# Staggered tile addresses: 160 bytes of padding behind activation and split-weight tiles in a two-layer decoder trunk

## The chip, the cores and the metric

The kernel runs on one core of a Trainium2 chip. The metric is the device time of one execution in microseconds (us); lower is better. Engines are named as the profile names them: PE is TensorE's matmuls, PEld its loads of the stationary operand, DVE is VectorE, ACT is ScalarE, POOL is GpSimd, and SP is the queue that issues most transfers.

## What is computed

The reference is a trunk of two decoder layers on 256 tokens of width 2048, in float32:

```python
for l in range(DEPTH):                      # DEPTH = 2
    h = _rmsnorm(x, norm1_g[l])
    if l % 2 == 0:
        x = x + _conv_diff_mixer(h, ...)    # projections to 6144 columns, conv, differential attention
    else:
        x = x + _fox_mixer(h, ...)          # 16 heads of 128, forgetting attention
    h = _rmsnorm(x, norm2_g[l])
    x = x + _sqrelu_mlp(h, mlp_w1[l], mlp_w2[l])   # hidden 8192
```

Nearly all work is matrix products of a 256-row activation with weights that are read once: a projection to 6144 columns, an output projection of 2048x2048, and an MLP of 2048x8192 and 8192x2048 in each layer.

## The kernel before

Every weight and every activation is used as a sum of two float32r numbers, a high part and a low part (float32r: the trace has one record for such a matmul, and two for one of plain float32). A product then takes three matmul terms: high by high, high by low and low by high. The tiles of interest are these:

- `act`: made in `ActT` (lines 103 to 111), 128 partitions by 4 k-tiles by {high, low} by 256 tokens, 8192 bytes in each partition. The pool `actp` has 9 buffers.
- `raw`: 8192 bytes of weights as they come from memory, 3 buffers, filled by SP's queue (lines 134, 136 and 517).
- `wh` and `wl`: the high and the low part of half a `raw`, 4096 bytes each, 4 buffers each. ACT makes `wh` by a copy that rounds (lines 142 and 524), DVE makes `wl` by a subtraction (lines 143 and 525).

Two routines do the products. `gemm` (lines 124 to 154) computes tokens by 512 output columns: the stationary operand is 128 columns of `act`, the moving operand is 512 columns of `wh` or `wl`, so lines 149, 150 and 151 are matmuls of 128x512. `gemm_t` (lines 510 to 536), used for the first product of each MLP, computes the transposed output: the stationary operand is 128 columns of `wh` (line 530) or `wl` (line 534), the moving operand is 512 columns of `act` (high and low side by side) or 256 columns of its high part. Each matmul is preceded by its own load of a 128x128 stationary operand, which runs while the matmul before it is still streaming.

Work that is not a product (norms, attention, convolution) is written as generators in the list `pending`; `step()` advances one of them after each half `raw`, and `until()` advances them until an activation is ready. This order is fixed when the program is built. A small product for the forget gates (`forget_gates`, lines 405 and 406) has slices of one constant tile `gws` as its stationary operand, which start 128 bytes apart.

Pools hand out addresses one behind the other. All larger tiles are multiples of 512 bytes long, so in the built program each `ident`, `xr`, `act`, `raw`, `wh`, `wl`, `q`, `k`, `v`, `junk`, `s` and `pT` starts at an address that is 128 modulo 512; `ones` and `triu` start at 32 modulo 512. The last tile ends at byte 227,648 of a partition, and the first 16,384 bytes are a scratch area for DMA descriptors that GpSimd would write.

Of the kernel before, what the change touches and what calls it, by code (L numbers as in the profile page):

```python
# [8 lines left out]
F32 = mybir.dt.float32  # L9
F32R = mybir.dt.float32r  # L10
# [6 lines left out]
P = 128  # L17
D = 2048
KT = D // P
CW = 512  # L20
# [6 lines left out]
def trunk_kernel(  # L27
# [7 lines left out]
    nc = tc.nc  # L35

    const = ctx.enter_context(tc.tile_pool(name="const", bufs=1))
    resid = ctx.enter_context(tc.tile_pool(name="resid", bufs=1))
    actp = ctx.enter_context(tc.tile_pool(name="actp", bufs=9))
    wraw = ctx.enter_context(tc.tile_pool(name="wraw", bufs=3))  # L40
    wspl = ctx.enter_context(tc.tile_pool(name="wspl", bufs=4))
# [8 lines left out]
    xr = [resid.tile([P, 2, CW], F32, name=f"xr{n}") for n in range(NCH)]  # L50
    xv = x[0].rearrange("(t p) d -> p t d", p=P)
    ident = const.tile([P, P], F32, name="ident")
    nc.scalar.dma_start(ident, eye)
    grow = work.tile([P, 2 * P], F32, name="y")[:32, :P]
    nc.sync.dma_start(grow, norm1_g.rearrange("l (k p) -> (l k) p", p=P))
# [21 lines left out]
    def step():  # L77

        while pending:
            try:  # L80
                next(pending[0])
                return True
            except StopIteration:
                pending.pop(0)
        return False

    def until(done):
        while not done():
            assert step()
# [13 lines left out]
    class ActT:  # L103


        def __init__(self, row):
            self.row = row
            self.left = 4
            self.both = actp.tile([P, 4, 2, 2 * P], F32R, name="act")
            self.hi = self.both[:, :, 0, :]  # L110
            self.lo = self.both[:, :, 1, :]

# [11 lines left out]
    def gemm(acts, w, c0, first=False):  # L124

        acc = [accp.tile([P, CW], F32, name="acc") for _ in range(2)]
        total = 4 * len(acts)
        i = 0
        for ai, a in enumerate(acts):
            raw = wraw.tile([P, 4, CW], F32, name="raw")  # L130
            src = w[a.row:a.row + CW, c0:c0 + CW].rearrange("(k p) n -> p k n", p=P)
            if first and ai == 0:
                for h in range(2):
                    nc.sync.dma_start(raw[:, 2 * h:2 * h + 2, :], src[:, 2 * h:2 * h + 2, :])
            else:
                nc.sync.dma_start(raw, src)
            until(lambda: a.left <= 0)
            for h in range(2):
                wh = wspl.tile([P, 2, CW], F32R, name="wh")
                wl = wspl.tile([P, 2, CW], F32R, name="wl")  # L140
                rw = raw[:, 2 * h:2 * h + 2, :]
                nc.scalar.copy(wh, rw)  # L142
                nc.vector.tensor_tensor(wl, rw, wh.bitcast(F32), ALU.subtract)  # L143
                for t in range(2):
                    ts = slice(t * P, (t + 1) * P)
                    for j in range(2):
                        k = 2 * h + j
                        st, sp = i + j == 0, i + j == total - 1
                        nc.tensor.matmul(acc[t], a.hi[:, k, ts], wh[:, j, :], start=st, stop=False)  # L149
                        nc.tensor.matmul(acc[t], a.hi[:, k, ts], wl[:, j, :], start=False, stop=False)  # L150
                        nc.tensor.matmul(acc[t], a.lo[:, k, ts], wh[:, j, :], start=False, stop=sp)  # L151
                i += 2
                step()
        return acc
# [36 lines left out]
    def proj(nm, w, c0, name, first=False):  # L191

        acc = gemm(nm.acts, w, c0, first)
        o = qkv.tile([P, 2, CW], F32, name=name)
        for t in range(2):
            nc.scalar.activation(o[:, t, :], acc[t], AF.Copy, scale=nm.r(t))
        return o
# [302 lines left out]
    def out_proj(acts, w, nxt):  # L500

        for part in (acts[:-1], acts[-1:]):
            for n in range(NCH):
                acc = gemm(part, w, n * CW)
                for t in range(2):
                    nc.vector.tensor_tensor(xr[n][:, t, :], acc[t], xr[n][:, t, :], ALU.add)
                if len(part) == 1:
                    pending.append(nxt.chunk(n))

    def gemm_t(acts, w, c0):  # L510


        acc = [accp.tile([P, CW], F32, name="acc") for _ in range(2)]
        for c in range(2):
            raw = wraw.tile([P, 8, 2 * P], F32, name="raw")
            r0 = c * 8 * P
            nc.sync.dma_start(raw, w[r0:r0 + 8 * P, c0:c0 + 2 * P].rearrange("(k p) n -> p k n", p=P))
            for h in range(2):
                a = acts[2 * c + h]
                until(lambda: a.left <= 0)  # L520
                wh = wspl.tile([P, 4, 2 * P], F32R, name="wh")
                wl = wspl.tile([P, 4, 2 * P], F32R, name="wl")
                rw = raw[:, 4 * h:4 * h + 4, :]
                nc.scalar.copy(wh, rw)  # L524
                nc.vector.tensor_tensor(wl, rw, wh.bitcast(F32), ALU.subtract)  # L525
                for f in range(2):
                    fs = slice(f * P, (f + 1) * P)
                    for k in range(4):
                        st = c + h + k == 0
                        nc.tensor.matmul(  # L530
                            acc[f], wh[:, k, fs], a.both[:, k, :, :].rearrange("p s t -> p (s t)"), start=st, stop=False)
                    for k in range(4):
                        sp = (c, h, k) == (1, 1, 3)
                        nc.tensor.matmul(acc[f][:, 2 * P:], wl[:, k, fs], a.hi[:, k, :], start=False, stop=sp)  # L534
                step()
        return acc

    def mlp(nm, l, nxt):
        ov = out[0].rearrange("(t p) d -> p t d", p=P)
        for g in range(4):  # L540
            hT = []
            for n in range(4):
                c0 = (4 * g + n) * CW
                a = ActT(c0)
                for i in range(2):
                    acc = gemm_t(nm.acts, mlp_w1[l], c0 + 2 * i * P)

                    r = work.tile([P, 2, 2 * P], F32, name="junk")
                    for f in range(2):
                        nc.scalar.copy(r[:, f, :], acc[f][:, 2 * P:])  # L550
                        nc.vector.tensor_tensor(r[:, f, :], acc[f][:, :2 * P], r[:, f, :], ALU.add)  # L551
                    nc.vector.scalar_tensor_tensor(r, r, 0.0, r, ALU.max, ALU.mult)  # L552
                    a.split((slice(None), slice(2 * i, 2 * i + 2)), r, None, 2)
                hT.append(a)
            if g == 0:
                r2 = small.tile([P, 2], F32, name="r2", bufs=3)
                for t in range(2):
                    nc.vector.tensor_tensor(r2[:, t:t + 1], nm.r(t), nm.r(t), ALU.mult)
            for n in range(NCH):
                acc = gemm(hT, mlp_w2[l], n * CW)  # L560
                for t in range(2):
                    nc.vector.scalar_tensor_tensor(  # L562
                        xr[n][:, t, :], acc[t], r2[:, t:t + 1], xr[n][:, t, :], ALU.mult, ALU.add)
                    if g == 3 and nxt is None:
                        q = nc.sync if t == 0 else nc.scalar
                        q.dma_start(ov[:, t, n * CW:(n + 1) * CW], xr[n][:, t, :])
                if g == 3 and nxt is not None:
                    pending.append(nxt.chunk(n))
# [11 lines left out]
    for g in range(2):  # L580
        q = proj(nm, w, 3 * C + g * CW, "q", first=g == 0)
        k = proj(nm, w, 4 * C + g * CW, "k")
# [16 lines left out]
    for g in range(4):  # L599
# [3 lines left out]
        k = proj(nm, w, D + g * CW, "k")  # L603
# [37 lines left out]
```

## Time and profile before

| | |
|---|---|
| Median of 3 runs | 2211.32 us (2210.77 to 2211.58) |
| Profiled execution: time / span of its instructions | 2211.69 us / 2210.0 us |
| PE busy, PEld busy | 100%, 84% of the span |
| DVE busy, ACT busy, POOL busy | 59%, 47%, 1% |
| Memory traffic | 412 MB, 186 GB/s |

The table is read as a statement about who could be late: an engine that is busy for the whole span leaves nothing for the others to delay, and then the question is how long its own instructions take. A matmul's duration in the profile includes its way through the array, so durations of successive matmuls overlap; what a matmul costs is the distance from its start to the next start, which the timeline view shows to 0.01 us.

### The profile page before, as it was taken

To read this page: it belongs to the slowest core of one execution; us is meant where nothing else is said; L and a number is where in the kernel's file an instruction comes from. 1 tells how busy PE (TensorE), PEld (TensorE's weight loads), DVE (VectorE), ACT (ScalarE), POOL (GpSimd) and SP (SyncE) were. 2 spreads that over 40 slices of the span, in tenths; PEclk is the share of its full clock that TensorE was granted. 3 is DMA by queue.
4 is the path that set the end of the run, shared out by engine and by line. 5 is a ranking of instruction groups with operands and counts; after the bars stand their busy time and mean duration, and the time that the engine had idled before them with its cause. 6 is when DMAs were issued, how large, how long until landed. Compare 5 with 4: busy or idle time off the path is not lost.

```text
span 2210.0 us, 26959 instructions
## 1 busy us (share of the span) xinstructions
PE 2199.4 (100%) x10868; PEld 1850.6 (84%) x10868; DVE 1293.1 (59%) x1608; ACT 1037.9 (47%) x1415; POOL 12.6 (1%) x17
## 2 busy tenths in 40 slices
PE   8999999999999999999999999999999999999999
PEld 7887888888888888888888888888888888888887
DVE  5676665655565565565556565666555655655654
ACT  6555544543443444344445455445434444444443
POOL 0000000000000000000000000000000000000000
PEclk9999999999999999999999999999999999999999
DMA  7554555665665665665555555555656656656664
GB/s 254 172 166 160 188 182 189 182 191 191 191 191 190 190 191 190 191 191 190 180 175 194 186 183 171 189 170 175 189 191 192 189 191 193 189 191 194 187 200 143
DMA packets 278015, 412.14 MB, mean 186 GB/s; under 512 B 9367, under 2 KB 144770, under 8 KB 277890
## 3 DMA queue, kind: packets, MB, share of 16 engines
q1 hardware_dynamic: 270032, 405.84, 58.2%
q10 hardware_dynamic: 7858, 4.58, 0.7%
q8 instruction: 85, 1.39, 0.3%
q14 instruction: 40, 0.33, 0.0%
HBM read 408.28 MB, written 2.11 MB: 186 GB/s over the span
## 4 chain that ended last, share of the span: by engine, by line
PE 99%; ACT 0%; DMA 0%; DVE 0%; SPq 0%; issue 0%
PE acc L530 22%; PE acc L149 21%; PE acc L151 21%; PE acc L150 21%; PE acc L534 11%; PE tp L170 1%; PE tp L286 0%; PE tp L298 0%; PE tp L474 0%; PE tp L494 0%; DMA xr<-in_x_dram 0%; PE tp L495 0%; PE tp L473 0%; PE tp L372 0%; PE tp L322 0%; PE tp L321 0%
## 5 line engine op out<-in xcount | busy, mean ns | idle before, releaser
L143 DVE TENSOR_TENSOR wl<-raw,wh 128x1024 fp32r<-128x1024 f32 x512 | 629.5, 1231 | 559.9 <-ACT wh L142 559.4
L142 ACT CAST wh<-raw 128x1024 fp32r<-128x1024 f32 x512 | 538.2, 1052 | 719.8 <-PE acc L151 637.0
L149 PE MATMUL acc<-wh,act 128*128 128x512 f32 x2048 | 812.9, 397 | 2.0 <-ACT wh L142 2.0
L151 PE MATMUL acc<-wh,act 128*128 128x512 f32 x2048 | 799.9, 391 | 0.0
L150 PE MATMUL acc<-wl,act 128*128 128x512 f32 x2048 | 798.7, 390 | 0.0
L530 PE MATMUL acc<-act,wh 128*128 128x512 f32 x2048 | 559.3, 394 | 0.0
L525 DVE TENSOR_TENSOR wl<-raw,wh 128x1024 fp32r<-128x1024 f32 x256 | 313.7, 1225 | 278.8 <-ACT wh L524 278.8
L151 PEld LDWEIGHTS acc<-wh,act 128*128 128x128 f32 x2048 | 385.0, 188 | 82.4
L149 PEld LDWEIGHTS acc<-wh,act 128*128 128x128 f32 x2048 | 385.2, 188 | 80.6 <-issue 2.7
L150 PEld LDWEIGHTS acc<-wl,act 128*128 128x128 f32 x2048 | 385.6, 188 | 77.2 <-DVE wl L143 0.8
L524 ACT CAST wh<-raw 128x1024 fp32r<-128x1024 f32 x256 | 269.0, 1051 | 328.3 <-PE acc L530 278.4
L530 PEld LDWEIGHTS acc<-act,wh 128*128 128x128 f32 x2048 | 350.4, 189 | 47.3
L534 PEld LDWEIGHTS acc<-act,wl 128*128 128x128 f32 x2048 | 314.2, 189 | 43.6
L534 PE MATMUL acc<-act,wl 128*128 128x256 f32 x2048 | 325.7, 281 | 0.0
L550 ACT COPY junk<-acc 128x256 f32<-128x256 f32 x128 | 47.3, 370 | 50.4 <-PE acc L534 50.4
L551 DVE TENSOR_TENSOR junk<-acc,junk 128x256 f32<-128x256 f32 x128 | 53.9, 421 | 0.0
L562 DVE SCALAR_TENSOR_TENSOR xr<-acc,r,xr 128x512 f32<-128x512 f32 x64 | 45.0, 743 | 7.8 <-PE acc L151 7.8
L552 DVE SCALAR_TENSOR_TENSOR junk<-junk 128x512 f32<-128x512 f32 x64 | 44.4, 693 | 2.2
L118 DVE TENSOR_TENSOR act<-junk,act 128x512 fp32r<-128x512 f32 x64 | 43.8, 685 | 0.0
L117 ACT CAST act<-junk 128x512 fp32r<-128x512 f32 x64 | 39.5, 617 | 0.0
L479 DVE SCALAR_TENSOR_TENSOR s<-ob,fc,tp 128x128 f32<-128x128 f32 (+1 forms) x32 | 11.8, 411 | 20.6 <-PE tp L474 20.6
L170 PE MATMUL tp<-ident,xr 128*128 128x128 f32 x128 | 20.3, 285 | 2.1 <-DMA xr<-in_x_dram 2.1
(145 smaller groups left out, 581.7 us busy)
## 6 DMA issues: line engine op xcount, KB each, us to landing
raw<-in_mlp_w_dram SPq DMA_DIRECT2D x256, 1024.0 KB, 5.4
raw<-in_fox_w_in_dram SPq DMA_DIRECT2D x48, 1024.0 KB, 5.1
raw<-in_hyb_w_in_dram SPq DMA_DIRECT2D x47, 1024.0 KB, 5.0
raw<-in_hyb_w_out_dram SPq DMA_DIRECT2D x16, 1024.0 KB, 5.0
raw<-in_fox_w_out_dram SPq DMA_DIRECT2D x16, 1024.0 KB, 5.0
ob<-fcd ACTq DMA_DIRECT2D x4, 512.0 KB, 3.7
xr<-in_x_dram SPq DMA_DIRECT2D x3, 512.0 KB, 7.2
raw<-in_hyb_w_in_dram SPq DMA_DIRECT2D x2, 512.0 KB, 5.9
```

The source lines that it names most:

```text
L142: nc.scalar.copy(wh, rw)
L143: nc.vector.tensor_tensor(wl, rw, wh.bitcast(F32), ALU.subtract)
L149: nc.tensor.matmul(acc[t], a.hi[:, k, ts], wh[:, j, :], start=st, stop=False)
L150: nc.tensor.matmul(acc[t], a.hi[:, k, ts], wl[:, j, :], start=False, stop=False)
L151: nc.tensor.matmul(acc[t], a.lo[:, k, ts], wh[:, j, :], start=False, stop=sp)
L524: nc.scalar.copy(wh, rw)
L525: nc.vector.tensor_tensor(wl, rw, wh.bitcast(F32), ALU.subtract)
L530: nc.tensor.matmul(acc[f], wh[:, k, fs], a.both[:, k, :, :].rearrange("p s t -> p (s t)"), start=st, stop=False)
L534: nc.tensor.matmul(acc[f][:, 2 * P:], wl[:, k, fs], a.hi[:, k, :], start=False, stop=sp)
L550: nc.scalar.copy(r[:, f, :], acc[f][:, 2 * P:])
L551: nc.vector.tensor_tensor(r[:, f, :], acc[f][:, :2 * P], r[:, f, :], ALU.add)
L562: nc.vector.scalar_tensor_tensor(xr[n][:, t, :], acc[t], r2[:, t:t + 1], xr[n][:, t, :], ALU.mult, ALU.add)
```

## The change

Tiles `act`, `wh` and `wl` get 40 float32 elements (160 bytes) that nobody reads or writes, so that successive buffers start 160 bytes further within 512. A tile of 384 bytes that nobody uses is put behind `ident`. The scratch area for DMA descriptors shrinks from 16,384 to 2048 bytes.

```diff
     ident = const.tile([P, P], F32, name="ident")
+    const.tile([P, 96], F32, name="pad")
...
-            self.both = actp.tile([P, 4, 2, 2 * P], F32R, name="act")
+            self.both = actp.tile([P, 16 * P + 40], F32R, name="act")[:, :16 * P].rearrange(
+                "p (k s t) -> p k s t", k=4, s=2)
...
-                wh = wspl.tile([P, 2, CW], F32R, name="wh")
-                wl = wspl.tile([P, 2, CW], F32R, name="wl")
+                wh = wspl.tile([P, 2 * CW + 40], F32R, name="wh")[:, :2 * CW].rearrange("p (j n) -> p j n", j=2)
+                wl = wspl.tile([P, 2 * CW + 40], F32R, name="wl")[:, :2 * CW].rearrange("p (j n) -> p j n", j=2)
...
-                wh = wspl.tile([P, 4, 2 * P], F32R, name="wh")
-                wl = wspl.tile([P, 4, 2 * P], F32R, name="wl")
+                wh = wspl.tile([P, 2 * CW + 40], F32R, name="wh")[:, :2 * CW].rearrange("p (k n) -> p k n", k=4)
+                wl = wspl.tile([P, 2 * CW + 40], F32R, name="wl")[:, :2 * CW].rearrange("p (k n) -> p k n", k=4)
...
-    nc = _bacc.Bacc("TRN2", target_bir_lowering=False, num_devices=1)
+    nc = _bacc.Bacc("TRN2", target_bir_lowering=False, num_devices=1, dynamic_dma_scratch_size=2048)
```

The addresses modulo 512 in the two built programs:

| Tile | before | after |
|---|---|---|
| `ident` | 128 | 128 |
| `xr` (4 tiles), `gws` | 128 | 0 |
| `act`, buffers 1 to 9 | 128 each | 0, 160, 320, 480, 128, 288, 448, 96, 256 |
| `raw`, 3 buffers | 128 each | 416 each |
| `wh`, buffers 1 to 4 | 128 each | 416, 64, 224, 384 |
| `wl`, buffers 1 to 4 | 128 each | 32, 192, 352, 0 |
| `q`, `k`, `v`, `junk`, `s`, `qkT`, `pT` | 128 each | 160 each |
| `ones`, `triu` | 32 | 416 |

The instructions of every engine, their shapes and their order are the same in both programs; only addresses differ.

## Rows read from the trace of the kernel before

**Rows 1.** The profile's page: span, busy time, share and instructions of each engine.
```profile
span 2210.0 us, 26959 instructions
PE 2199.4 (100%) x10868; PEld 1850.6 (84%) x10868; DVE 1293.1 (59%) x1608; ACT 1037.9 (47%) x1415; POOL 12.6 (1%) x17
```

**Rows 2.** The page's chain that ended last, by engine; granted clock by slices (tenths).
```profile
PE 99%; ACT 0%; DMA 0%; DVE 0%; SPq 0%; issue 0%
PEclk9999999999999999999999999999999999999999
```

**Rows 3.** Timeline of PE in `gemm`, 340 to 351.5 us; start, us, engine, line.
```profile
339.78 0.39 PE L151 MATMUL acc<-wh,act 128*128 128x512 f32 x1
340.01 0.39 PE L149 MATMUL acc<-wh,act 128*128 128x512 f32 x1
340.24 0.39 PE L150 MATMUL acc<-wl,act 128*128 128x512 f32 x1
340.46 0.39 PE L151 MATMUL acc<-wh,act 128*128 128x512 f32 x1
...
351.34 0.39 PE L151 MATMUL acc<-wh,act 128*128 128x512 f32 x1
```

**Rows 4.** Timeline of PE in `gemm_t`, 999.6 to 1002.6 us.
```profile
999.68 1.09 PE L530 MATMUL acc<-act,wh 128*128 128x512 f32 x4
1000.61 0.63 PE L534 MATMUL acc<-act,wl 128*128 128x256 f32 x4
1001.08 1.09 PE L530 MATMUL acc<-act,wh 128*128 128x512 f32 x4
1002.01 0.64 PE L534 MATMUL acc<-act,wl 128*128 128x256 f32 x4
1002.49 0.40 PE L530 MATMUL acc<-act,wh 128*128 128x512 f32 x1
```

**Rows 5.** The page's groups: line, engine, tiles, shapes, count | busy us, mean ns | idle.
```profile
L149 PE MATMUL acc<-wh,act 128*128 128x512 f32 x2048 | 812.9, 397 | 2.0 <-ACT wh L142 2.0
L534 PE MATMUL acc<-act,wl 128*128 128x256 f32 x2048 | 325.7, 281 | 0.0
```

**Rows 6.** Timeline of PE at a plain float32 matmul pair in the attention.
```profile
1207.02 0.59 PE L494 MATMUL tp<-pT,v 128*128 128x256 f32 x2
1207.45 0.38 PE L495 MATMUL tp<-pT,v 128*128 128x128 f32 x2
```

**Rows 7.** DMA queues (packets, MB, share of 16 engines) and the largest issue.
```profile
q1 hardware_dynamic: 270032, 405.84, 58.2%
q10 hardware_dynamic: 7858, 4.58, 0.7%
raw<-in_mlp_w_dram SPq DMA_DIRECT2D x256, 1024.0 KB, 5.4
```

**Rows 8.** Groups and waits around the weight split: ACT, DVE, who waited for whom.
```profile
L143 DVE TENSOR_TENSOR wl<-raw,wh 128x1024 fp32r<-128x1024 f32 x512 | 629.5, 1231 | 559.9 <-ACT wh L142 559.4
L142 ACT CAST wh<-raw 128x1024 fp32r<-128x1024 f32 x512 | 538.2, 1052 | 719.8 <-PE acc L151 637.0
ACT wh L142 <- PE acc L151: 637.0, 399, 3.6
```

**Rows 9.** Single lines: instructions of L149, L530, L534, durations ns min/median/max.
```profile
L149 PE MATMUL acc<-wh,act x2048: 387/389/796, 9.1 to 2205.5; 128*128 128x512 f32 x187
L530 PE MATMUL acc<-act,wh x2048: 387/396/481, 393.8 to 2118.3; 128*128 128x512 f32 x187
L534 PE MATMUL acc<-act,wl x2048: 274/280/285, 394.8 to 2118.9; 128*128 128x256 f32 x187
```

**Rows 10.** Timeline of PE at the forget gates' product with slices of `gws`.
```profile
1133.28 0.28 PE L405 MATMUL tp<-act,gws 128*128 128x256 f32 x1
1133.39 0.29 PE L406 MATMUL tp<-act,gws 128*128 128x256 f32 x1
...
1133.88 0.29 PE L406 MATMUL tp<-act,gws 128*128 128x256 f32 x1
1134.01 0.28 PE L405 MATMUL tp<-act,gws 128*128 128x256 f32 x1
...
1135.18 0.40 PE L149 MATMUL acc<-wh,act 128*128 128x512 f32 x1
```

**Rows 11.** Timeline of PE where `triu` is loaded for the forget gates.
```profile
1153.24 0.39 PE L149 MATMUL acc<-wh,act 128*128 128x512 f32 x1
1153.47 0.39 PE L150 MATMUL acc<-wl,act 128*128 128x512 f32 x1
1153.69 0.40 PE L151 MATMUL acc<-wh,act 128*128 128x512 f32 x1
1153.93 0.29 PE L442 MATMUL tp<-flf,triu 128*128 128x16 f32 x2
```

## The prediction, made before the changed kernel was run

> **What bounds the kernel now.** I read the page's busy times first. PE is busy for 2199.4 of 2210.0 us [rows 1], and in the chain that ended last 99% lies on PE, with nothing on DMA, DVE or ACT [rows 2]. The granted clock is nine tenths or more in every slice, its upper level of 2.4 GHz. So the time can only move if PE's own instructions come closer together, or if another engine grows until PE has to wait for it.
>
> The next view is the timeline of PE, because a matmul's listed duration is not its cost. In `gemm` 52 matmuls of 512 columns start from 339.78 to 351.34 us; the last is the 52nd from the row at 339.78 on, so the distance from start to start is 11.56 us / 51 = 226.7 ns [rows 3]. At 2.4 GHz 512 columns take 512 / 2.4 = 213.3 ns. In `gemm_t` eight matmuls of 512 columns take 0.93 + 0.93 us, 232.5 ns each, and eight of 256 columns take 0.47 + 0.48 us, 118.75 ns each, against 106.7 ns of streaming [rows 4]. So each of 10,240 matmuls (5 lines of 2048, as in [rows 5]) costs 10 to 20 ns more than its columns need.
>
> Where may that come from? The plain float32 pair of line 494 streams 256 columns in 0.43 / 2 us = 215 ns each [rows 6]: twice the time for the same columns, so the moving operand is read at half the pace, with the same 128x128 load of the next stationary operand running beside it. There the distance is within 2 ns of 213.3. Only where the moving operand comes at full pace beside a load is there an excess. This is what two readers that get in each other's way would show, and in this kernel both readers' addresses agree modulo 512 nearly everywhere, which the change ends.
>
> **The change part by part.**
>
> *Smaller scratch, the tile "pad".* No instruction is added, and the order on all engines stays. Transfers run on two queues of the hardware kind, 58.2% and 0.7% of the engines' time [rows 7], so a scratch area for GpSimd's descriptors is not used: cost 0, no cover needed.
>
> *`raw` starts at 416 instead of 128 modulo 512.* The trace has no transfer to such an address. If its packets became slower, they would have to take 1 / 0.58 = 1.7 times as long before the queues were full; a load lands 5.4 us after its issue [rows 7], and three buffers hold 24 matmuls each, 24 x 226.7 ns = 5.4 us per buffer. I take 0; if the cover went, PE would wait for `wh` through ACT.
>
> *ACT and DVE on shifted tiles.* For each half `raw` ACT takes 1.05 us and DVE 1.23 us [rows 8], against 12 matmuls x 226.7 ns = 2.7 us on PE. ACT's largest wait is for PE to give a `wh` back, 637.0 us in 399 waits [rows 8]; it is ahead of PE. Either could take twice as long before PE noticed. I take 0, whichever way their durations go.
>
> *The matmul distance.* This is the only term. The trace has no matmul of a large group at other offsets, so it is bounded from both sides.
>
> Best side: no excess of contention at all, the pace of line 494, 215 ns, and half of it, 107.5 ns, for 256 columns. `gemm`: 3 lines x 2048 = 6144 matmuls x (226.7 - 215) = 72 us; line 530: 2048 x (232.5 - 215) = 36 us; line 534: 2048 x (118.75 - 107.5) = 23 us. Sum 131 us, time 2081 us.
>
> Between: the best spacing that occurs in the lines themselves. Durations move with the spacing: the median of line 149 is 389 ns at a spacing of 226.7, its smallest is 387; line 530 has a median of 396 at 232.5 and a smallest of 387; line 534 has 280 at 118.75 and 274 [rows 9]. If all matmuls stood at their line's smallest: 6144 x 2 + 2048 x 9 + 2048 x 6 ns = 12 + 18 + 12 = 43 us, time 2169 us. These numbers come about at equal offsets, by different histories before the matmul, so better meetings of the two readers exist.
>
> Worst side: the spacing of line 530 for all of `gemm` too. 6144 x (232.5 - 226.7) = 36 us, time 2247 us.
>
> I take half of what separates today's spacing from the best one seen, 21.5 us: with 9, 4 and 4 different offsets the readers meet in many ways, some of them as good as the best, some as now. Against the profiled execution's own 2211.69 us (1.69 us of it outside the span of 2210.0, unchanged; it stands 0.4 us above the median of the three runs) this gives **2190 us**, 1.0% faster.
>
> Here a rule speaks against the change. The row: 226.7 ns at full pace, 215 ns at half pace, each beside a load [rows 3, 6]. The Trainium skill, page "TensorE: Matmul & The Clock Gate", section "Part 2: What happens when you issue a matmul", says that PE has two independent read ports, and that loading the next weights "doesn't steal SBUF read bandwidth from the running matmul". By that, no offset can matter and the sum is 0, time 2211; the same page's section "Back-to-back issue gap" gives N / 2.4 + 2.5 ns, 215.8 ns for 512 columns, an estimate that the half-pace row agrees with and the full-pace row does not.
>
> **The rivals.**
>
> *Addresses do not matter (or only below 32 bytes, which the change leaves alone): 2211 us.* The excess would be a price of the load itself, whatever it reads. For it: the forget gates' product uses slices of `gws` that start 128 bytes apart, so that four relative offsets occur; its 16 matmuls of 256 columns take 1135.18 - 1133.28 = 1.90 us, 118.75 ns each [rows 10], just what line 534 has at equal offsets. Against it: within these 16 the spacing changes (0.11 us from the first to the second, 0.13 us where 1133.88 goes to 1134.01), and the load of `triu` below.
>
> *The lock is lost: 2247 us.* In `gemm` the spacing is a steady 226.7 ns over dozens of matmuls; in `gemm_t`, where groups of four 512s and four 256s alternate, it never settles and is 232.5. A steady state that forms because all tiles are at the same offset would be broken by the change: `wh` and `wl` are another pair of buffers every 12 matmuls, with another distance to `act` each time. Price: 36 us, worked out above. For it speaks the one matmul of the large groups that runs beside a load from another offset (`triu`, 32 modulo 512, the moving operand at 128): from 1153.69 to 1153.93 are 0.24 us where 0.22 and 0.23 stand before it [rows 11], some 10 ns too much. It decides against the change as soon as the mean spacing in `gemm` is over 226.7 by more than what `gemm_t` gains, that is if 6144 matmuls lose more than a third of what 2048 + 2048 win. If all 8192 matmuls of 512 columns lost those 10 ns, it would be 82 us, 2294 us, the end of this case.
>
> *The conflict goes altogether: 2081 to 2169 us.* For it: only the pairing of full pace and load shows an excess [rows 3, 4, 6]. Against it: the four offsets of `gws`, none of which is rid of the excess on the mean [rows 10].
>
> *The change does not do what it says* can be set aside: the built program has the offsets in the table ahead. What remains open is whether 512 is the length that counts, and that is within the first rival.
>
> **How the numbers follow.** A measurement of this kernel tells about 0.2%, 4.4 us, from no change. Partial gain, 2169 to 2207 us: 0.33, the likeliest, and it gives the time. Altogether gone, 2081 to 2169 us: 0.09. Same: 0.26. Lock lost, 2216 to 2294 us with its middle at 2247: 0.32, a little under the partial gain because the trace has only one load that speaks for it; most of it lies under 2255. So faster 0.42, same 0.26, slower 0.32. Cases of both signs hold much of the chance; the likeliest one's own range is 2169 to 2207. To hold 8 in 10 the range reaches up past the lost lock's 2247 to 2255, leaving some 0.09 above it, and down to 2140, into the case in which the conflict goes, leaving some 0.06 below.
>
> **What would show it.** In the changed kernel's timeline, a stretch of `gemm` in which starts lie 222 to 226 ns apart on the mean, with different values for different buffers of `wh`, would show the term right; in `gemm_t` the four matmuls of line 530 should take less than 0.93 us. The medians of lines 149, 150 and 151 should come apart from each other, since 149 and 151 stream `wh` and 150 streams `wl`, at other offsets. If all distances stay at 226.7, 232.5 and 118.75, the first rival holds; if `gemm` stands at 230 or more, the lock was lost. PE should stay busy for 99% or more, with ACT still waiting for PE; if `wh` or a DMA shows up as a releaser of PE, my covers were wrong. The prediction fails in sign if durations of line 149 are 393 ns or more at their median.

## The result, and the profile after

The changed kernel takes 2235.93 us (median of 4 runs, 2235.49 to 2236.71), the kernel before took 2211.05 us beside it: a ratio of 1.0113, 95% interval 1.0095 to 1.013. It is 24.9 us **slower**. The stated range held the time, the sign was forecast wrongly. One of the ten executions of the first experiment's kernel took 7856 us, for a reason that its record does not show; it is left out of that kernel's ratio, and all other executions of every kernel lie within 0.1% of their median.

The page of the changed kernel answers to [rows 1, 2, 5] (its lines stand two further down in the file, so line 149 is now 151, 530 is 532 and 534 is 536):

```profile
span 2234.1 us, 26959 instructions
...
PE 2223.3 (100%) x10868; PEld 1849.7 (83%) x10868; DVE 1293.4 (58%) x1608; ACT 1035.4 (46%) x1415; POOL 12.2 (1%) x17
...
PE 99%; DMA 0%; SPq 0%; ACT 0%; DVE 0%; issue 0%
...
L151 PE MATMUL acc<-wh,act 128*128 128x512 f32 x2048 | 820.9, 401 | 3.0 <-ACT wh L144 3.0
L153 PE MATMUL acc<-wh,act 128*128 128x512 f32 x2048 | 807.4, 394 | 0.0
L152 PE MATMUL acc<-wl,act 128*128 128x512 f32 x2048 | 806.6, 394 | 0.0
L532 PE MATMUL acc<-act,wh 128*128 128x512 f32 x2048 | 558.5, 394 | 0.0
```

The same instructions as before, PE busy for the whole span, and the chain still on PE alone: the 24.1 us that the span grew by are longer distances between matmuls, not waits. The timeline of PE in `gemm`, 344 to 356 us (start, us, engine, line), answers to [rows 3]:

```profile
343.83 0.40 PE L151 MATMUL acc<-wh,act 128*128 128x512 f32 x1
344.07 0.40 PE L152 MATMUL acc<-wl,act 128*128 128x512 f32 x1
344.30 0.40 PE L153 MATMUL acc<-wh,act 128*128 128x512 f32 x1
...
355.90 0.39 PE L152 MATMUL acc<-wl,act 128*128 128x512 f32 x1
```

The last row is the 53rd: 12.07 us / 52 = 232.1 ns from start to start, where 226.7 stood. Over the whole trace, leaving out the 2.5 in a hundred matmuls with 260 ns or more to the next, the mean spacing in `gemm`, worked out from the trace's start times, went from 227.5 to 231.7 ns. 6144 x 4.2 ns = 26 us; with nothing left out, the distances in `gemm` add up to 1440.2 us where they were 1415.4, 24.8 us more: that is all of the loss. In `gemm_t` it is 231.9 ns for 512 columns and 118.5 for 256, against 232.2 and 118.5: nothing. The durations of single lines (min/median/max ns), beside [rows 9], say the same; the last line is line 150 of the kernel before:

```profile
L151 PE MATMUL acc<-wh,act x2048: 387/394/797, 9.5 to 2229.6; 128*128 128x512 f32 x187
L152 PE MATMUL acc<-wl,act x2048: 388/393/792, 10.8 to 2229.9; 128*128 128x512 f32 x187
L153 PE MATMUL acc<-wh,act x2048: 387/393/628, 11.3 to 2230.1; 128*128 128x512 f32 x187
L532 PE MATMUL acc<-act,wh x2048: 387/393/482, 398.5 to 2140.5; 128*128 128x512 f32 x187
L536 PE MATMUL acc<-act,wl x2048: 274/280/290, 399.6 to 2141.0; 128*128 128x256 f32 x187
```

```profile
L150 PE MATMUL acc<-wl,act x2048: 387/389/796, 10.4 to 2205.7; 128*128 128x512 f32 x187
```

The three lines of `gemm` moved their medians from 389 to 393 and 394; the smallest value, 387, still occurs, but rarely. Counted over all 6144 matmuls of `gemm`, 387 or 388 ns became more frequent (431, before 94), but 392 ns and more far more so (4734, before 939). The covers held, as first the waits (us in total, times, longest) and then the DMA queue (packets, MB, share) show beside [rows 7, 8]:

```profile
ACT wh L144 <- PE acc L153: 660.4, 399, 3.6
```

```profile
q1 hardware_dynamic: 270032, 405.84, 57.4%
```

ACT waits for PE a little longer than before, and `raw` at 416 modulo 512 did not make the transfers longer.

### The profile page after: what moved, and what is told of

The parts are those of the page before. It is cut to its first block, busy times and chain, and to the rows that moved or that the text cites. A ratio compares the mean times of both kernels' runs of the same rounds, so it can differ in the third digit from the quotient of the medians.

```text
span 2234.1 us, 26959 instructions
## 1 busy us (share of the span) xinstructions
PE 2223.3 (100%) x10868; PEld 1849.7 (83%) x10868; DVE 1293.4 (58%) x1608; ACT 1035.4 (46%) x1415; POOL 12.2 (1%) x17
## 4 chain that ended last, share of the span: by engine, by line
PE 99%; DMA 0%; SPq 0%; ACT 0%; DVE 0%; issue 0%
PE acc L151 21%; PE acc L153 21%; PE acc L152 21%; PE acc L532 21%; PE acc L536 11%; PE tp L172 1%; PE tp L288 0%; PE tp L300 0%; PE tp L476 0%; PE tp L496 0%; DMA raw<-in_hyb_w_in_dram 0%; PE tp L497 0%; PE tp L475 0%; PE tp L374 0%; PE tp L324 0%; PE tp L323 0%
```

## The experiments

In what follows "distance" is the address of `wh` and `wl` minus that of `act`, in bytes. All kernels have the small scratch, and the order of the instructions stays. "Spacing" is from start to start, as a mean over the trace without distances of 260 ns or more.

### The parts without the spread

```diff
+    const.tile([P, 96], F32, name="pad")
+    ... dynamic_dma_scratch_size=2048
```

> Only the small scratch and the 384-byte tile, no padding in act, wh and wl: all of them at 0 modulo 512. Theory L (the steady 226.7 ns of gemm needs tiles whose distances modulo 512 do not change, the change broke it): 2211 us, median duration 389 ns on the three lines of gemm. Theory A (absolute addresses, or where raw lies, or the scratch, made the change slower): 2220 us or more. Within 2 us of 2211 settles it against A for these parts.

Measured: 2211.24 us, ratio 1.000 (0.999 to 1.001). Scratch and extra tile cost nothing, and neither does moving all tiles together from 128 to 0 modulo 512.

### Only the weights spread

```diff
-                wh = wspl.tile([P, 2, CW], F32R, name="wh")
+                wh = wspl.tile([P, 2 * CW + 40], F32R, name="wh")[:, :2 * CW].rearrange("p (j n) -> p j n", j=2)
```

The same for `wl` and for the two tiles of `gemm_t`.

> Only wh and wl are padded by 160 bytes, act stays at 128 modulo 512: eight different distances instead of up to sixteen. Theory L: the lock goes as in the full change, 2232 to 2238 us, gemm 231 to 232 ns from start to start. If what hurts is the spread of act alone: 2211 us. Half the loss (2223 us) would say that both spreads add.

Measured: 2232.28 us, ratio 1.0094 (1.0079 to 1.0109); `gemm` 231.2 ns, `gemm_t` 232.3 and 117.7. Most of the loss (21 of 25 us) comes with the weights alone. Theory L, that the short spacing needs distances that stay the same, stood so far.

### One distance for all, 32 bytes

```diff
+    gap = ctx.enter_context(tc.tile_pool(name="gap", bufs=1))
+    gap.tile([P, 8], F32, name="gap")
     wspl = ctx.enter_context(tc.tile_pool(name="wspl", bufs=4))
```

> No padding in the tiles; a 32-byte tile ahead of wh and wl puts all eight of them at 160 modulo 512 while act stays at 128: one distance for all matmuls, but not 0. Theory L (sameness makes the lock): 2211 us, 226.7 ns in gemm. Theory Z (distance 0 is what is good, any other meets worse): 2225 to 2250 us, as single distances in the changed kernel have 230 to 234 ns. Under 2205 us would say that a distance chosen well beats 0.

Measured: 2245.4 us, ratio 1.0155 (1.0139 to 1.017): slower than the changed kernel itself, with no variety of offsets at all. PE in `gemm`, 340 to 351.5 us:

```profile
339.65 0.40 PE L151 MATMUL acc<-wh,act 128*128 128x512 f32 x1
339.89 0.39 PE L152 MATMUL acc<-wl,act 128*128 128x512 f32 x1
340.12 0.40 PE L153 MATMUL acc<-wh,act 128*128 128x512 f32 x1
...
351.32 0.40 PE L153 MATMUL acc<-wh,act 128*128 128x512 f32 x1
```

The last row is the 51st: 11.67 / 50 = 233.4 ns. The pattern is as steady as the one before, only at a longer spacing: the distances repeat 235, 233, 234, 231 ns, where 226, 227, 227 repeated. Theory L fell here: it is not sameness that gives 226.7 ns.

### Padding that keeps the offset modulo 512

```diff
-            self.both = actp.tile([P, 4, 2, 2 * P], F32R, name="act")
+            self.both = actp.tile([P, 16 * P + 128], F32R, name="act")[:, :16 * P].rearrange(
+                "p (k s t) -> p k s t", k=4, s=2)
```

`wh` and `wl` get 128 elements in the same way.

> act, wh and wl padded by 512 bytes each: the tiles move apart and change modulo 1024 and above, but all stay at 128 modulo 512. Theory L and Z with 512 as the length that counts: 2211 us. If larger address bits count too, or padding as such costs: 2220 us or more.

Measured: 2211.7 us, ratio 1.0002 (0.9992 to 1.0011), 227.5 ns. Padding as such is free, and whole steps of 512 bytes do not count.

### Other single distances: 64, 128, 256, 192 and 16 bytes

The tile `gap` above gets 16, 32, 64 and 48 elements; for 16 bytes the tiles are padded by 512 bytes and used from their fifth element on (`[:, 4:2 * CW + 4]`).

> As the kernel with one distance of 32 bytes, with 64 bytes instead: wh and wl at 192, act at 128 modulo 512. Theory Z (every distance has a price of its own, 0 is good): about 230 ns in gemm, as loads at this distance have in the changed kernel (448 modulo 512: mean 230.0), so 2225 to 2235 us. Theory P (the pattern repeats within 64 bytes, so 64 is as good as 0): 2211 us.

> One distance of 128 bytes: wh and wl at 256, act at 128 modulo 512. Theory Z: 230.5 to 233 ns in gemm (loads at 384 modulo 512 have 230.6 in the changed kernel, 233.2 in the one with padded weights alone), 2230 to 2248 us. Theory P with a period of 128 bytes: 2211 us.

> One distance of 256 bytes: wh and wl at 384, act at 128 modulo 512. Theory Z with 512 as the length that counts: 231 ns in gemm, about 2235 us. Theory P with a period of 256 bytes: 2211 us. Under 2205 us would be a distance that beats 0.

> wh and wl begin 16 bytes inside a tile padded by 512 bytes, so all of them lie at 144, act at 128 modulo 512. Theory Z: another price than at 0, between 2211 and 2245 us, and not 2211. If only steps of 32 bytes count: 2211 us.

> One distance of 192 bytes: wh and wl at 320, act at 128 modulo 512, which is 64 as gemm counts it (stationary minus moving) and 192 as gemm_t counts it, the mirror of the kernel with 64 bytes. Theory Z in its symmetric form (only the size of the distance counts): 2214 us, 229 ns in gemm and 114.6 ns for 256 columns. If the sign counts: other values, somewhere between 2205 and 2245 us.

| Distance, bytes | Time, us | Ratio, 95% interval | `gemm`, ns | `gemm_t` 512, ns | `gemm_t` 256, ns |
|---|---|---|---|---|---|
| 0 (before) | 2211.3 | 1 | 227.5 | 232.2 | 118.5 |
| 16 | 2237.76 | 1.012 (1.0103 to 1.0137) | 231.7 | 233.5 | 118.2 |
| 32 | 2245.4 | 1.0155 (1.0139 to 1.017) | 233.2 | 231.5 | 119.3 |
| 64 | 2214.18 | 1.0013 (1.0003 to 1.0022) | 229.3 | 232.1 | 114.6 |
| 128 | 2242.46 | 1.0141 (1.0126 to 1.0156) | 232.6 | 233.4 | 117.7 |
| 192 | 2236.57 | 1.0113 (1.0098 to 1.0129) | 233.3 | 230.4 | 115.6 |
| 256 | 2211.37 | 1.000 (0.999 to 1.0009) | 227.5 | 232.2 | 118.5 |
| mixed (the change) | 2235.93 | 1.0113 (1.0095 to 1.013) | 231.7 | 231.9 | 118.5 |

256 bytes give the kernel before again in all three spacings: the length that counts is 256, not 512, as far as 0 and 256 can tell; no other two single distances that lie 256 apart were tried. Theory P with that period holds and with shorter ones falls; theory Z holds for single distances. The kernel with 64 bytes missed its expectation of 2225 to 2235 us all the same: `gemm` lost some 11 us (6144 x 1.8 ns), but the matmuls of 256 columns won 8 (2048 x 3.9 ns), which had not been reckoned with. Nor does a distance's price carry over whole to a mixture. In the trace of the kernel with only the weights spread, taking the buffers in the pool's order, matmuls in `gemm` that stream a buffer at distance 0, 32 or 128 have 228.1, 233.2 and 233.2 ns, near the single values, but 64 and 192 have 231.0 and 229.1, the other way round. The last step that tells relative from absolute: all tiles moved together by 128 cost nothing (2211.24 us), the weights moved by 128 against `act` cost 31 us. So it is the distance. The weights also moved against `raw`, which ACT and DVE read while they write `wh` and `wl`; but at 128 bytes the spacing in `gemm` is 232.6 ns both beside a busy and beside an idle ACT, and 232.8 and 232.5 ns beside DVE, so the work of these two is not what costs. Since `gemm` has `act` stationary and `gemm_t` has it moving, 64 and 192 are each other's mirror; they differ (229.3 against 233.3 ns in `gemm`), so the sign counts too. The two distances' groups of lines, for 64 and then for 192 bytes:

```profile
L151 PE MATMUL acc<-wh,act 128*128 128x512 f32 x2048 | 815.0, 398 | 2.0 <-ACT wh L144 2.0
L532 PE MATMUL acc<-act,wh 128*128 128x512 f32 x2048 | 558.9, 395 | 0.0
L536 PE MATMUL acc<-act,wl 128*128 128x256 f32 x2048 | 318.0, 277 | 0.0
```

```profile
L151 PE MATMUL acc<-wh,act 128*128 128x512 f32 x2048 | 822.7, 402 | 2.7 <-ACT wh L144 2.7
L532 PE MATMUL acc<-act,wh 128*128 128x512 f32 x2048 | 555.4, 393 | 0.0
L536 PE MATMUL acc<-act,wl 128*128 128x256 f32 x2048 | 319.7, 278 | 0.0
```

Before, lines 149 and 534 had 812.9 and 325.7 us [rows 5], and line 530 had 559.3:

```profile
L530 PE MATMUL acc<-act,wh 128*128 128x512 f32 x2048 | 559.3, 394 | 0.0
```

Line 536 is the one row that both distances make better by more than 1 us, by 7.7 and 6.0 us, and 192 also takes 3.9 us off line 532. What is lost lies in `gemm`.

### Another distance in `gemm_t` than in `gemm`

`gemm_t` uses the same buffers and can begin further on in them. First with `wl` alone, 64 bytes on:

```diff
-                wl = wspl.tile([P, 4, 2 * P], F32R, name="wl")
+                wl = wspl.tile([P, 2 * CW + 64], F32R, name="wl")[:, 16:2 * CW + 16].rearrange("p (k n) -> p k n", k=4)
```

> wh and wl padded by 256 bytes (which alone changes nothing by the run at one distance of 256); gemm uses them from the tile's start, gemm_t uses wl from 64 bytes further on. So gemm keeps distance 0 and the loads of line 534 get distance 64. Theory Z with 256 as the length that counts: gemm stays at 227.5 ns, the 256-column spacing falls from 118.5 to about 114.6 as in the kernel with 64 bytes for all, 2048 x 3.9 ns = 8 us: 2203 us, faster than both kernels. If the 114.6 came from wh at distance 64 and not from wl: 2211 us.

Measured: 2209.53 us, ratio 0.9991 (0.9981 to 1.0), no difference that this measurement tells. `gemm` kept 227.5 ns, but the spacing of 256 columns was 118.3 and not 114.6, though three of the four loads beside these streams, those of `wl`, had the same distance as in the kernel with 64 bytes for all. The fourth, of `wh`, is not the reason: at the second and third matmul of the four, where both the matmul's own load and the next are of `wl`, the spacing is 117.4 and 117.5 ns where the kernel with 64 bytes for all has 113.4. A matmul's spacing depends on what ran before it too.

Then both tiles, 192 bytes on (`[:, 48:2 * CW + 48]`):

> Tiles wh and wl padded by 256 bytes; gemm uses both from the start (distance 0), gemm_t uses both from 192 bytes further on, as it had it in the kernel with 192 bytes for all (230.35 and 115.59 ns against 232.2 and 118.51 before). Theory Z: gemm stays at 227.5 ns, gemm_t brings 2048 x (1.85 + 2.92) ns = 9.8 us: 2201 to 2203 us, faster than both kernels. If what gemm_t gains is lost in the change between the two offsets: 2209 to 2211 us, as with wl alone.

Measured: **2201.78 us** (2201.66 to 2202.38, 5 runs), ratio 0.9957 (0.9944 to 0.9971): 9.5 us faster than the kernel before and 34 us faster than the changed one. Spacings 227.5, 230.3 and 115.6 ns. In its `gemm_t`, beside [rows 4]:

```profile
998.93 1.09 PE L530 MATMUL acc<-act,wh 128*128 128x512 f32 x4
999.86 0.62 PE L534 MATMUL acc<-act,wl 128*128 128x256 f32 x4
1000.31 1.07 PE L530 MATMUL acc<-act,wh 128*128 128x512 f32 x4
1001.22 0.63 PE L534 MATMUL acc<-act,wl 128*128 128x256 f32 x4
1001.70 1.09 PE L530 MATMUL acc<-act,wh 128*128 128x512 f32 x4
```

Two groups of eight take 1001.70 - 998.93 = 2.77 us, where 2.81 stood. Over 256 such pairs that is the gain.

### Shorter loads

Is the excess over 213.3 ns what the load beside the stream reads? Three kernels make the load half as long. Their matmuls also fill only half of the output's rows, so what they compute is incomplete: the first leaves out half of the term low by high, the other two half of nearly all of `gemm`.

```diff
-                        nc.tensor.matmul(acc[t], a.lo[:, k, ts], wh[:, j, :], start=False, stop=sp)
+                        m = P if sp else P // 2
+                        nc.tensor.matmul(acc[t][:m], a.lo[:, k, t * P:t * P + m], wh[:, j, :], start=False, stop=sp)
```

> The third product term of gemm (line 151) is computed for 64 of 128 tokens of each half, except in the last matmul of a sum: its load of the stationary operand is 64 columns instead of 128, and it still streams 512 columns. Tiles lie as before. If the excess over 213.3 ns is taken from the stream by the reads of the load beside it (theory R): the spacing from line 150 to line 151, beside whose stream the half load runs, falls by about half of its excess of 13.4 ns, to 219 to 222 ns, and the time by some 12 us to about 2199 us. If the excess is a fixed price per matmul (theory F): spacing 227 ns, 2211 us.

Measured: 2226.14 us, ratio 1.0068 (1.0051 to 1.0084). The load's listed duration fell from 188 to 134 ns, the spacing beside it rose to 229.2 ns, and to 230.0 and 230.9 beside the full loads. Neither theory R nor F said so. Since every third load was now of another length, the steady state may just have gone, so the next kernels halve all three terms, at distance 0 and 32:

> All three product terms of gemm are computed for 64 of 128 tokens of each half, except in the first and the last matmul of a sum: nearly all loads in gemm are 64 columns, all alike, and each matmul still streams 512 columns. Distance 0 as before. Theory R (the excess is made by what the load reads while the stream runs; with all loads alike the steady state can form): 213.3 + 13.4 / 2 = 220 ns, time 2211 - 6144 x 6.7 ns = 2170 us. Theory F (a price per matmul, whatever the load's length): 226.7 ns, 2211 us; or 2226 us and more if the phase between the two is what counts.

> The same with one distance of 32 bytes for wh and wl. Theory R: the 20 ns of excess at this distance halve too, 223 ns in gemm, some 18 us over the kernel with half loads at distance 0. Theory F: as the full loads at 32 bytes, 233 ns, 2245 us.

Measured: 2225.61 us (1.0064, 1.0046 to 1.0083) and 2231.91 us (1.0093, 1.0074 to 1.0111); 230.0 and 231.0 ns in `gemm`. The load and the matmul of the third term at distance 0 (durations min/median/max ns), first in the kernel with that one term halved, then in the kernel before:

```profile
L152 PEld LDWEIGHTS acc<-wh,act x2048: 133/134/232, 10.6 to 2219.7; 128*64 128x64 f32 x173, 128*128 128x128 f32 x14
L152 PE MATMUL acc<-wh,act x2048: 387/393/628, 11.0 to 2219.9; 128*64 128x512 f32 x173, 128*128 128x512 f32 x14
```

```profile
L151 PEld LDWEIGHTS acc<-wh,act x2048: 187/188/338, 10.5 to 2205.7; 128*128 128x128 f32 x187
L151 PE MATMUL acc<-wh,act x2048: 388/389/632, 10.9 to 2205.9; 128*128 128x512 f32 x187
```

At distance 0 a load of half the length makes the matmul no quicker on the mean; at 32 bytes it does, 231.0 ns against 233.2, far from the 223 of theory R. A steady state did form: with all three terms halved at distance 0 the distances repeat 230, 236, 229, 224, 227, 234 ns, which is 230.0 on the mean. Theory R in this form is refuted: the excess is not so many nanoseconds for each element that the load reads. Theory F's 226.7 and 233 ns were not met either; of the cases named ahead, 2226 us and more "if the phase between the two is what counts" is the nearest to 2225.61, but that figure was known from the run before, so it is no support. What the half-filled output does to the spacing was not tested by itself. With short loads the distance counts less: 32 bytes cost 1.0 ns instead of 5.7.

## Why the prediction was wrong

**What bounds the kernel** was read rightly: all of the difference is in the spacing of PE's matmuls, and the three terms set to 0 (scratch and extra tile, `raw` at another offset, ACT and DVE on shifted tiles) are 0 in the runs.

**The step that failed** is the size taken for "the matmul distance": "with 9, 4 and 4 different offsets the readers meet in many ways, some of them as good as the best, some as now". It measured 4.2 ns more in `gemm` where the sum has 1 ns saved, and in `gemm_t` 0.3 ns and nothing saved where it has 4.5 and 3: 24.9 us lost instead of 21.5 won. The sum counts meetings from the best one seen up to today's and none that is worse than today's. The single distances show that for `gemm` equal offsets are the best of the six that were tried modulo 256: 227.5 ns, against 229.3 to 233.3. The change's offsets give all multiples of 32 as distances, 0 among them, and its 231.7 ns lies among the single values. That the mixture is a weighted mean of them is not shown, since prices change beside other distances. The range held the time only because it was drawn up to 2255 to cover the rival of the other sign, not by the mechanism that gave the forecast.

The smallest durations in [rows 9] were read as "better meetings" to be had. In `gemm` of the kernel before they were passing values: behind other matmuls its distances run, for example from 143.2 us on, 314, 235, 233, 236, 224, 231 ns and so on, and settle at 226 and 227 after some ten matmuls. In the changed kernel such short ones did become more frequent, as the result shows, but the long ones outnumber them by far. A minimum seen in passing does not say how often a change will meet it.

**The rival "the lock is lost"** had sign, place and nearly the size: 2247 was worked out from the spacing of line 530, 232.5 ns, and `gemm` came to 231.7, so 2236. The prediction's own sign of being wrong, 393 ns or more as the median of line 149, came true with 394. It named too little of the cause, though. The steady spacing does not need "all tiles at the same offset": at a single distance of 32 bytes it is as steady, at 233.4 ns. What takes equal offsets, modulo 256 as far as tried, is the short spacing of 226.7 ns.

**The one row that spoke for it**, the load of `triu` [rows 11], pointed the right way. `triu` lay 96 bytes under the moving operand, and beside its load the distance was 235 ns in a single instance, where it is 228 beside the first loads of lines 473 and 494, of plain float32 too but at equal offsets; I gave it little weight beside the mean of `gws` [rows 10]. That mean said "no difference" for a reason that the runs show: slices 128 bytes apart have, modulo 256, only the distances 0 and 128, and those were matmuls of 256 columns, whose spacing at 128 bytes is 117.7 ns against 118.5 in `gemm_t`, while 512 columns in `gemm` lose 5.1 ns there.

**The rival "addresses do not matter"** is refuted by 16 bytes (26 us) as by 128 (31 us). The Trainium skill says on the page "TensorE: Matmul & The Clock Gate", section "Part 2: What happens when you issue a matmul", that a load of the next weights does not take SBUF read bandwidth from the running matmul. As the prediction read it, that no offset can matter, it does not hold here: the measured spacing depends on where the load's operand lies against the stream's, by up to 5.8 ns in `gemm`. Whether it is read bandwidth that is lost, no run shows. **The rival "the conflict goes altogether"** is refuted for all distances tried: none comes near 215 ns.

**Not settled:** what in the chip repeats every 256 bytes, and what the excess of 13 ns at the best distance consists of. Half loads, at which it should have halved, left 230.0 ns. Distances of 96, 160 and 224 bytes as single values, and a spread of `act` alone, were not tried. That the load and the stream are the two readers that meet is argued, not shown: every matmul here has a load beside it.

## What to carry to other kernels

When matmuls follow each other without a gap, measure their distance from start to start, per line, before touching the layout: it shows an address effect of 1 to 2% that an engine's busy share and the chain that ended last do not show. Tiles of stationary and moving operands that lie at the same offset are not by that in each other's way; here it was the best case tried for one routine, and spreading addresses was a loss. Try single distances one by one, with padding as the only edit, and per routine, since here the best one for `gemm` was 0 and the best one for `gemm_t` 192, and since a spacing depends on what ran just before.

## What the runs showed of the hardware

- The spacing of this kernel's float32r matmuls depends on the distance between the stationary and the moving operand, and on its sign (64 and 192 bytes: 229.3 and 233.3 ns in `gemm`). 0, 256 and padding by 512 give 227.5 ns, the other distances tried up to 233.3. Moving both operands together by 128 bytes does nothing (2211.24 us).
- It has a memory: with the matmul's own load and the next both at 64 bytes, the spacing of 256 columns was 113.4 or 117.5 ns, depending on the distance in the four matmuls before.
- Halving the columns of the load, and with them the rows of the output, at full length of the stream, made the mean spacing at distance 0 longer (230.0 against 227.5 ns) and at 32 bytes shorter (231.0 against 233.2).
